# Full-width small operations in the norms, wider copies in S5, and a planner that looks 2000 operations ahead

## The chip, the cores and the metric

One core of a Trainium2 chip runs the whole program. The metric is the device time of one execution in microseconds (us); less is better. TensorE (PE) multiplies matrices out of SBUF into PSUM, which has eight banks of 128 partitions by 512 float32 values; VectorE (DVE), ScalarE (ACT) and GpSimd (POOL) do elementwise work on either memory; SyncE (SP) issues the DMA transfers. PE's weight loads have a line of their own, PEld.

## What is computed

Two blocks for a sequence of 512 tokens with 1024 features, in float32. The first is NSA attention (compressed, selected and windowed) beside retention, then a squared-ReLU feed-forward. The second is modulated by a condition vector (six gates out of `w_ada`), mixes with mLSTM beside an S5 state-space model, and ends with a gated feed-forward. What the change touches, cut from the reference:

```python
def rms_norm(x, w):
    xf = x.astype(jnp.float32)
    y = xf * lax.rsqrt(jnp.mean(xf * xf, axis=-1, keepdims=True) + EPS)
    return (y * w.astype(jnp.float32)).astype(x.dtype)

def _standardize(x):
    xf = x.astype(jnp.float32)
    mu = jnp.mean(xf, axis=-1, keepdims=True)
    var = jnp.mean(jnp.square(xf - mu), axis=-1, keepdims=True)
    return ((xf - mu) * lax.rsqrt(var + LN_EPS)).astype(x.dtype)

def _hybrid_mixer(h, ...):
    ...
    hm = _mlstm_chunkwise(q, k, v, ip.transpose(0, 2, 1), fp.transpose(0, 2, 1))
    hm = _standardize(hm).transpose(0, 2, 1, 3).reshape(Bsz, S, MLSTM_WIDTH).astype(h.dtype)
    y_a = (hm * mlstm_norm_gain * jax.nn.sigmoid(om)) @ w_mlstm_down
    ys = jax.nn.gelu(_s5_ssm(us, ...))
    ...

def _s5_ssm(u, ...):
    ...
    _, _, xr, xi = lax.associative_scan(combine, (a_r, a_i, bu_r, bu_i), axis=1)
    y = jnp.einsum('gcp,bsgp->bsgc', c_re, xr) - jnp.einsum('gcp,bsgp->bsgc', c_im, xi)
    y = y.reshape(Bsz, S, W) + d * uf
```

## The kernel before, in words

Activations lie with features on the partitions and tokens along the row: eight tiles `x` of 128 features by 512 tokens, worked on in halves `hf` of 256 tokens. A product in float32 is made as three products of rounded parts (`xh`, `xl` against `w` and its remainder); their matmuls write the PSUM tiles `ps_g`. Other PSUM tiles are `ps_s`, `ps_t` (transposes and broadcasts) and `ps_o`; all come from one pool of eight banks.

The program is not issued in the order in which it is written. A class `Order` records every operation with its dependences, and `flush` runs a list scheduler (`simulate`) several times with different priorities, each engine taking the most urgent of its operations that are ready; the best order is then issued engine by engine. What sets the order is therefore a table of costs: `time` (duration of an operation by engine, width and number of one-column operands), `shares` (whether DVE and POOL exclude one another in it), `region` (which part of a tile an operation touches) and `AHEAD`: no operation is issued that lies more than `AHEAD` places beyond the first one that is still to be issued. Since all operations are issued in one place, each has the same line, L519, and is told apart by its tiles.

The places that matter here:

- `newton` computes a reciprocal square root on DVE from an integer estimate and three steps. `rsqrt` scales its input. Results and temporaries are called `r..y`, `r..a`, `r..t`, with `rl` in the layer norms, `r1` and `r3` in the RMS norms, `rm` in mLSTM, `rq` and `rk` in the head norms. For four columns or fewer, every step is one operation for each column.
- A layer norm needs the mean over the partitions. `token_means` multiplies by a `mean` matrix into `ps_s`, copies the result to `tm` and transposes it; `add_up` has added most of the eight tiles (`ssum`, `lsum`) and of their squares (`sq`) before, but not tiles 6 and 7, so four tiles go through the `mean` matmuls. Then DVE copies the means (`lm`), forms the variance (`lw`, `lv`) and the root `rly`, and PE transposes `lm` and `rly` (the transposes `ps_t<-cf,lm` and `ps_t<-cf,rly`) into rows that DVE and POOL apply to `x`.
- `standardize2` does two layer norms at once from the sums of six quantities (`wsel`, `wrow`, then `wa`): first mean and root, then a second mean `wm`, variance `wv` and root. PE meets two roots in each half.
- `mlstm_head` copies numerator and denominator of each of four row blocks out of `ps_o` into `nm`, normalizes by `md`, and standardizes `nm` with the root `rmy`; PE then transposes `nm`.
- The end of S5: for each of four quarters, eight small matmuls `ps_o<-U,s5k` and eight matmuls with a block-diagonal operand, `ps_o<-s5z,wraw`. POOL zeroes `s5z`; DVE copies the states `X` into its diagonal blocks, 32 values on 64 partitions at a time. `X` itself comes out of PSUM earlier by `X<-ps_o`. DVE also computes a one-column `gb`, which ACT needs for `om`, mLSTM's output gate.
- `raw`: the 48 loads of `w_ada` and the DVE products with the condition, `raw<-raw,silu`.

Of the kernel before, what the change touches and what calls it, by code (L numbers as in the profile page):

```python
# [15 lines left out]
I32 = mybir.dt.int32  # L16
# [7 lines left out]
AHEAD = 800  # L24
# [151 lines left out]
class Order:  # L176
# [41 lines left out]
    def region(ap, t):  # L218

        if t.psum:  # L220
            return 0, 128, 0, 1
# [9 lines left out]
    def add(self, engine, fn, args, kw):  # L231
        i, deps, use = len(self.ops), set(), {}
        for a, w in [(a, n == 0) for n, a in enumerate(args)] + [(a, k == "accum_out") for k, a in kw.items()]:
# [4 lines left out]
            r, keep = self.region(a, t), []  # L238
# [10 lines left out]
    def time(self, engine, fn, args, kw):  # L249
# [5 lines left out]
        cols = sum(self.width(a) == 1 for a in aps[1:]) if wide > 1 else 0  # L255
# [9 lines left out]
        if engine == "vector":  # L265
            return 68 + wide * (6.25 if fn == "reciprocal" else 1.042) + 61 * cols + 60 * ("accum_out" in kw)
# [23 lines left out]
    def shares(self, op):  # L290
# [231 lines left out]
class Kern:  # L522
# [1808 lines left out]
```

## Time and profile before

| | before |
|---|---|
| median of 3 runs (lowest, highest) | 1505.81 us (1504.4, 1506.77) |
| profiled execution | 1505.45 us |
| its span, from first to last instruction | 1503.3 us |
| mean granted clock of PE | 0.991 |
| PE, DVE, ACT, POOL busy | 97%, 75%, 46%, 38% of the span |
| chain that ended last | PE 86%, DVE 10%, DMA 2%, ACT 1% |

The span is what the trace covers; the rest of the execution's time lies around it. A share of busy time is a mean over stages that differ. [...] "Idle before" is the time in which an engine stood still before an instruction, with the one that released it.

### The profile page before, as it was taken

The numbers are of one execution on the slowest core, as the hardware profiler recorded it, in microseconds if no ns is written. First come the engines' busy times: TensorE is split into PE (matmuls) and PEld (weight loads), VectorE is DVE, ScalarE is ACT, GpSimd is POOL, SyncE is SP. The second block draws the span as 40 slices with busy tenths as digits, with TensorE's granted clock in tenths as the row PEclk, the third lists the DMA queues.
The fourth block names the chain that finished last, engine by engine and source line by source line (L and its number), as shares of the span: only waits on it lengthen the run. The fifth ranks groups of instructions, "written<-read, shape, count | busy, mean of one in ns | idle before, by whom it ended". The sixth has DMA issues, their size and how long they took to land.

```text
span 1503.3 us, 24351 instructions
## 1 busy us (share of the span) xinstructions
PE 1461.9 (97%) x8738; PEld 1221.4 (81%) x8738; DVE 1124.8 (75%) x2641; ACT 688.6 (46%) x1397; POOL 569.8 (38%) x583
## 2 busy tenths in 40 slices
PE   9999999999999999999999899999999999999996
PEld 6779656888888777899778777878888899998996
DVE  6896798998974674565887863656488999897886
ACT  6454465444333333453563354434265555454553
POOL 6332334240060660143186102120127357464635
PEclk9999999999999999999999899999999999999998
DMA  6731114858731533415313543345311133323331
GB/s 218 224 108 64 56 43 160 267 193 279 235 116 42 176 129 119 153 46 176 107 57 100 158 137 124 119 147 180 143 63 51 50 106 99 116 88 106 100 97 57
DMA packets 81065, 188.34 MB, mean 125 GB/s; under 512 B 18352, under 2 KB 28528, under 8 KB 80944
## 3 DMA queue, kind: packets, MB, share of 16 engines
q1 hardware_dynamic: 80944, 186.78, 38.5%
q8 instruction: 69, 1.13, 0.3%
q14 instruction: 52, 0.43, 0.1%
HBM read 168.70 MB, written 15.17 MB: 122 GB/s over the span
## 4 chain that ended last, share of the span: by engine, by line
PE 86%; DVE 10%; DMA 2%; ACT 1%; issue 1%; POOL 0%; SPq 0%; ACTq 0%; DVEq 0%; POOLq 0%
PE ps_g L519 72%; PE ps_s L519 6%; PE ps_o L519 5%; PE ps_t L519 3%; DVE s5z L519 1%; DVE w L519 1%; DVE x L519 1%; DVE rlt L519 1%; DMA wraw<-in_w_fg_dram 1%; DVE rly L519 0%; DVE r3t L519 0%; DVE rmt L519 0%; DMA wraw<-in_w_f_dram 0%; DVE r3y L519 0%; DMA wraw<-in_w_down_dram 0%
## 5 line engine op out<-in xcount | busy, mean ns | idle before, releaser
L519 DVE TENSOR_TENSOR w<-wraw,w 128x512 fp32r<-128x512 f32 (+2 forms) x390 | 321.3, 837 | 92.2 <-ACT w L519 87.8
L519 ACT ACTIVATE w<-wraw 128x512 fp32r<-128x512 f32 (+1 forms) x398 | 240.3, 609 | 318.0 <-PE ps_g L519 248.6
L519 PE MATMUL ps_g<-xsh,w 128*128 128x256 f32 (+1 forms) x1088 | 278.8, 338 | 2.6 <-DVE w L519 2.2
L519 PE MATMUL ps_g<-xh,w 128*128 128x512 f32 x736 | 240.2, 398 | 0.0
L519 PEld LDWEIGHTS ps_g<-xsh,w 128*128 128x128 f32 x1088 | 188.6, 190 | 28.7 <-DVE w L519 2.6
L519 PE MATMUL ps_g<-xsl,w 128*128 128x256 f32 (+1 forms) x544 | 182.6, 336 | 0.0
L519 PEld LDWEIGHTS ps_g<-xh,w 128*128 128x128 f32 x736 | 137.7, 188 | 33.6 <-issue 1.9
L519 PE MATMUL ps_g<-xl,w 128*128 128x512 f32 x368 | 145.9, 397 | 0.0
L519 PE MATMUL ps_g<-mdh,w 128*128 128x512 f32 (+1 forms) x480 | 143.7, 374 | 0.1
L519 POOL TENSOR_TENSOR x<-x,lc 128x256 f32<-128x256 f32 x72 | 52.6, 773 | 185.9 <-ACT lc L519 173.7
L519 PEld LDWEIGHTS ps_g<-xsl,w 128*128 128x128 f32 x544 | 103.3, 190 | 11.0
L519 PE MATMUL ps_g<-tfh,w 128*128 128x256 f32 x576 | 107.5, 281 | 0.9 <-DVE wo L519 0.4
L519 PEld LDWEIGHTS ps_g<-mdh,w 128*128 128x128 f32 x480 | 87.1, 188 | 17.9 <-issue 0.8
L519 PE MATMUL ps_g<-fmh,w 128*128 128x512 f32 (+1 forms) x332 | 101.4, 375 | 0.0
L519 PEld LDWEIGHTS ps_g<-tfh,w 128*128 128x128 f32 x576 | 89.7, 188 | 2.1 <-DVE wo L519 0.9
L519 PE MATMUL ps_g<-mdl,w 128*128 128x512 f32 (+1 forms) x240 | 89.6, 373 | 0.0
L519 PEld LDWEIGHTS ps_g<-xl,w 128*128 128x128 f32 x368 | 69.2, 188 | 15.6
L519 PE MATMUL ps_g<-tfl,w 128*128 128x256 f32 x288 | 78.0, 281 | 0.0
L519 POOL TENSOR_TENSOR ws<-wraw 128x512 f32<-128x512 f32 x36 | 57.1, 1591 | 51.7 <-DMA wraw<-in_w_fv_dram 27.2
L519 DVE SCALAR_TENSOR_TENSOR raw<-raw,silu 128x1024 f32<-128x1024 f32 x48 | 62.7, 1305 | 9.7 <-DMA raw<-in_w_ada_dram 9.2
L519 PEld LDWEIGHTS ps_g<-fmh,w 128*128 128x128 f32 x332 | 59.8, 188 | 10.3 <-issue 0.2
L519 DVE TENSOR_TENSOR w<-ws,w 128x512 fp32r<-128x512 f32 x72 | 58.7, 829 | 11.1 <-ACT w L519 10.8
(510 smaller groups left out, 3471.1 us busy)
## 6 DMA issues: line engine op xcount, KB each, us to landing
raw<-in_w_ada_dram SPq DMA_DIRECT2D x48, 512.0 KB, 4.3
wraw<-in_w_dram SPq DMA_DIRECT2D x36, 512.0 KB, 3.7
wraw<-in_w_up_dram SPq DMA_DIRECT2D x32, 512.0 KB, 4.2
wraw<-in_w_down_dram SPq DMA_DIRECT2D x32, 512.0 KB, 3.7
wraw<-in_w_fv_dram SPq DMA_DIRECT2D x22, 512.0 KB, 3.9
wraw<-in_w_fg_dram SPq DMA_DIRECT2D x22, 512.0 KB, 3.7
wraw<-in_w_f_dram SPq DMA_DIRECT2D x14, 512.0 KB, 4.3
wraw<-in_w_fd_dram SPq DMA_DIRECT2D x16, 384.0 KB, 3.1
```

Source lines behind the costliest of these rows:

```text
L519: getattr(getattr(self.nc, op.engine), op.fn)(*op.args, **op.kw)
```

## The change

1. The planner: `AHEAD` goes from 800 to 2000. Dependences through a PSUM bank are kept by the whole bank for PE alone and by ranges for the other engines. One-column operations with column operands are planned at a higher cost, others at a lower one, and `shares` no longer exempts one-column operations or those that write PSUM.
2. `newton` always works on the full width, 11 operations in a row, and holds its value in PSUM (`room`): the upper half of the bank that `token_means` transposed into, the bank of the six sums in `standardize2`, or one more bank in `head_factors` and `mlstm_head`.
3. `standardize2` works on both columns at once with an operand in PSUM, and takes one square on ACT. mLSTM's `md` is formed for each row block, from PSUM.
4. `add_up` adds tiles 6 and 7 as well, so that two tiles, not four, go through the `mean` matmuls: 32 fewer on PE (8381 before, 8349 after), and two more additions for each sum on DVE or POOL.
5. S5: 64 copies of 64 values that are written next to each other take the place of 128 copies of 32 values written 32 bytes apart; the 8 memsets of 128x512 become 16 of 64x256. PE now reads `U` in steps of 32 bytes, and `s5z` in runs of eight values; ACT writes its result `y` in steps of eight values.

In instructions, DVE goes from 2595 to 2286, POOL from 588 to 604, ACT from 1335 to 1339 and its table loads from 4 to 6; SP's transfers are 492 in both.

```diff
 SLOTS = 70
-AHEAD = 800
+AHEAD = 2000
 NEG = -1.0e30
...
     @staticmethod
-    def region(ap, t):
-
-        if t.psum:
-            return 0, 128, 0, 1
+    def region(ap, t, bank=True):
+
+        if t.psum and bank:
+            return 0, 128, 0, S
         dims, o = [(int(s), int(c)) for s, c in ap.ap], int(ap.offset)
...
 
-        cols = sum(self.width(a) == 1 for a in aps[1:]) if wide > 1 else 0
+        cols = sum(self.width(a) == 1 for a in aps[1:]) if wide > 1 else sum(hasattr(a, "tensor") for a in (
+            args[2:4] if fn == "tensor_scalar" else args[2:3] if fn == "scalar_tensor_tensor" else kw.values()))
         if engine == "tensor":
...
             return len(aps) > 0
-        if op.engine != "vector" or any(a.tensor.name in self.psum for a in [op.args[0], *aps]):
+        if op.engine != "vector" or any(a.tensor.name in self.psum for a in aps):
             return False
-        one = self.width(op.args[0]) == 1
-        return op.fn in ("tensor_tensor", "scalar_tensor_tensor") or op.fn in ("tensor_scalar", "tensor_copy") and not one
+        return op.fn in ("tensor_tensor", "scalar_tensor_tensor") or op.fn in ("tensor_scalar", "tensor_copy") and op.args[0].tensor.name not in self.psum
 
...
         V = self.nc.vector
-        y, a, t = (self.small(name + c, n, bufs) for c in "yat")
-        if n <= 4:
-
-            y_, a_, t_, v_ = ([x[:, j:j + 1] for j in range(n)] for x in (y, a, t, v))
-            for j in range(n):
-                V.tensor_scalar(y_[j].bitcast(I32), v_[j].bitcast(I32), -0.5, float(0x5F3759DF), op0=OP.mult, op1=OP.add)
-                V.tensor_scalar(a_[j], v_[j], -0.5, None, op0=OP.mult)
-            for i in range(3):
-                for j in range(n):
-                    V.tensor_scalar(t_[j], y_[j], y_[j], a_[j], op0=OP.mult, op1=OP.mult)
-                for j in range(n):
-                    V.tensor_scalar(y_[j], t_[j], 1.5, y_[j], op0=OP.add, op1=OP.mult)
-            if post:
-                for j in range(n):
-                    V.tensor_scalar(y_[j], y_[j], post, None, op0=OP.mult)
-            return y
+        out, a, t = (self.small(name + c, n, bufs) for c in "yat")
+        y = self.room[:, 0:n]
         V.tensor_scalar(y.bitcast(I32), v.bitcast(I32), -0.5, float(0x5F3759DF), op0=OP.mult, op1=OP.add)
         V.tensor_scalar(a, v, -0.5, None, op0=OP.mult)
-        for _ in range(3):
-            V.tensor_tensor(t, y, y, op=OP.mult)
-            V.tensor_tensor(t, t, a, op=OP.mult)
-            V.scalar_tensor_tensor(y, t, 1.5, y, op0=OP.add, op1=OP.mult)
+        for i in range(3):
+            V.tensor_tensor(t, a, y, op=OP.mult)
+            V.tensor_tensor(t, t, y, op=OP.mult)
+            V.scalar_tensor_tensor(out if i == 2 and not post else y, t, 1.5, y, op0=OP.add, op1=OP.mult)
         if post:
-            V.tensor_scalar(y, y, post, None, op0=OP.mult)
-        return y
+            V.tensor_scalar(out, y, post, None, op0=OP.mult)
+        return out
 
...
         T.transpose(pt[:, 0:128], t, self.ident)
+        self.room = pt[:, 256:512]
         return pt[:, 0:128].rearrange("p (q r) -> p q r", r=32)[:, :, 0]
...
         n = st.n
+        self.room = self.bank("t")
 
...
         e = (self.nc.gpsimd, self.nc.vector)[k % 2]
-        if 1 < k < 6:
+        if k > 1:
             e.tensor_tensor(s[k % 2][:, c], (x[k - 2] if k < 4 else s[k % 2])[:, c], x[k][:, c], op=OP.add)
         self.nc.scalar.activation(q[k][:, c], x[k][:, c], AF.Square)
-        if 1 < k < 6:
+        if k > 1:
             e.tensor_tensor(q[k % 2][:, c], q[k % 2][:, c], q[k][:, c], op=OP.add)
...
             T.matmul(pv[:, 6 * j:6 * j + 6], rows[:, 128 * j:128 * j + 128], st.sel, start=j == 0, stop=True, skip_group_check=True)
-        a = self.small("wa", 12, 2).rearrange("p (n j) -> p n j", j=2)
-        V.tensor_copy(a, pv[:, 0:12].rearrange("p (j n) -> p n j", j=2))
-        m, s1, s2, s3, q, q2 = (a[:, n] for n in range(6))
+        m0, s1, s2, s3, q, q2 = (pv[:, 0:12].rearrange("p (j n) -> p n j", j=2)[:, n] for n in range(6))
+        m = self.small("wa", 2, 2)
+        V.tensor_copy(m, m0)
         c1, c2, c3, c4 = (st.cs[:, n:n + 1] for n in range(4))
-        v = self.small("wv", 2, 2)
-        each_ = lambda *vs: [[u[:, j:j + 1] for u in vs] for j in range(2)]
-        for m_, v_, q_ in each_(m, v, q):
-            V.tensor_scalar(v_, m_, m_, -1.0, op0=OP.mult, op1=OP.mult)
-        for m_, v_, q_ in each_(m, v, q):
-            V.tensor_scalar(v_, v_, 1e-5, q_, op0=OP.add, op1=OP.add)
+        v, t = self.small("wv", 2, 2), self.small("wt", 2, 2)
+        self.room = pv[:, 256:512]
+        V.scalar_tensor_tensor(v, m0, -1.0, m, op0=OP.mult, op1=OP.mult)
+        V.scalar_tensor_tensor(self.room[:, 2:4], q, 1e-5, v, op0=OP.add, op1=OP.add)
         mb = self.columns(m)
...
         A.activation(mc, mb, AF.Copy)
-        r = self.newton(v, 2, "rl")
-
-        for m_, a1, a2, a3, p_ in each_(m, s1, s2, s3, q2):
-            V.tensor_scalar(a1, m_, c1, a1, op0=OP.mult, op1=OP.subtract)
-            V.tensor_scalar(a3, m_, c3, a3, op0=OP.mult, op1=OP.subtract)
-            V.tensor_scalar(a2, m_, c2, a2, op0=OP.mult, op1=OP.subtract)
-            V.tensor_scalar(p_, a2, m_, p_, op0=OP.mult, op1=OP.add)
-            V.tensor_scalar(p_, a1, a1, p_, op0=OP.mult, op1=OP.subtract)
+        r = self.newton(self.room[:, 2:4], 2, "rl")
+
+        V.scalar_tensor_tensor(s1, m, c1, s1, op0=OP.mult, op1=OP.subtract)
+        V.scalar_tensor_tensor(s3, m, c3, s3, op0=OP.mult, op1=OP.subtract)
+        V.scalar_tensor_tensor(v, m, c2, s2, op0=OP.mult, op1=OP.subtract)
+        A.activation(t, s1, AF.Square)
+        V.tensor_tensor(s2, v, m0, op=OP.mult)
+        V.tensor_tensor(v, t, s2, op=OP.subtract)
+        V.tensor_tensor(q2, q2, v, op=OP.subtract)
         for k in range(8):
...
             A.activation(nm[i], po[:, 0:257], AF.Copy)
+            V.scalar_tensor_tensor(d0[:, i:i + 1], po[:, 256:257], -1.0, nm[i][:, 256:257], op0=OP.mult, op1=OP.max)
             st = self.small("bst", 6, 2)
...
 
-        d, e = self.small("md", 4, 2), self.small("me", 4, 2)
-        for i, t in enumerate(n2):
-            dn = t[:, :, 256]
-            V.scalar_tensor_tensor(d[:, 2 * i:2 * i + 2], dn, -1.0, dn, op0=OP.mult, op1=OP.max)
-        V.tensor_tensor(d, d, self.em[:, :, h], op=OP.max)
-        V.tensor_tensor(d, d, d, op=OP.mult)
+        self.room = self.bank("t")
+        d, e = self.room[:, 8:12], self.room[:, 4:8]
+        for t in (d, dm):
+            V.tensor_tensor(t, d0, self.em[:, :, h], op=OP.max)
+        V.tensor_tensor(d, d, dm, op=OP.mult)
         V.scalar_tensor_tensor(e, d, 1e-5, mv[:, :, 1], op0=OP.mult, op1=OP.add)
-        r = self.rsqrt(e, 4, 1.0, 0.0, "rm")
+        r = self.newton(e, 4, "rm")
         for i in range(4):
...
                 o = ps[:, 64 * g:64 * g + 64]
-                T.matmul(o, kk[g], self.U[q][:, g, :], start=g == 0, stop=False, skip_group_check=True)
+                T.matmul(o, kk[g], self.U[q][:, g, :].rearrange("p (s j) -> p j s", j=8), start=g == 0, stop=False, skip_group_check=True)
             for i in range(2):
-                x = self.t2("s5z", F32, (128, 4, 2, 64))
-                G.memset(x, 0.0)
+
+                x = self.t2("s5z", F32, (128, 2, 8, 4, 8))
                 for e in range(2):
                     r = slice(64 * e, 64 * e + 64)
+                    G.memset(x[r, 1 - e], 0.0)
                     for n in range(4):
-                        for j in range(2):
-                            V.tensor_copy(x.rearrange("p g e (s j) -> p j e g s", j=8)[r, 2 * n + j, e],
-                                          self.X[n][r, j, :, i, 4 * q:4 * q + 4].rearrange("p s g -> p g s"))
+                        V.tensor_copy(x[r, e, 2 * n:2 * n + 2], self.X[n][r, :, :, i, 4 * q:4 * q + 4].rearrange("p j s g -> p j g s"))
                 for g in range(4):
-                    T.matmul(ps[:, 128 * g:128 * g + 128], m[:, i, g, :], x[:, g].rearrange("p e k -> p (e k)"),
+                    T.matmul(ps[:, 128 * g:128 * g + 128], m[:, i, g, :], x[:, :, :, g, :],
                              start=False, stop=i == 1, skip_group_check=True)
             y = self.t2("y5")
-            A.activation(y, ps, AF.Copy)
+            A.activation(y.rearrange("p (g s j) -> p g j s", g=8, s=8), ps.rearrange("p (g j s) -> p g j s", g=8, j=8), AF.Copy)
             nc.sync.dma_start(yd[q].rearrange("s c g k -> (s c) (g k)"), y)
```

The change also moves instructions. Three places follow, the rows of one engine before and after, in the order in which they are issued; "x" at a row's end counts like rows in succession.

DVE at the end of one of mLSTM's heads and of S5, before: the last step of the root `rmy`, the scaling of `nm`, then copies into `s5z`, with `gb` behind 58 of them.

```order
L519 TENSOR_SCALAR rmy<-rmt,rmy 128x1 x4
L519 TENSOR_SCALAR nm<-nm,mv,rmy 128x256 x4
L519 COPY s5z<-X 64x4x8 x58
L519 TENSOR_SCALAR gb<-nw_899 128x1
L519 COPY s5z<-X 64x4x8 x2
L519 SCALAR_TENSOR_TENSOR om<-om,ps_t 128x512
L519 COPY s5z<-X 64x4x8 x2
```

The same place in the changed kernel.

```order
L521 COPY s5z<-X 64x64
L521 TENSOR_TENSOR rmt<-rma,ps_t 128x4
L521 TENSOR_SCALAR gb<-nw_894 128x1
L521 TENSOR_TENSOR rmt<-rmt,ps_t 128x4
L521 SCALAR_TENSOR_TENSOR ps_t<-rmt,ps_t 128x4
...
L521 SCALAR_TENSOR_TENSOR rmy<-rmt,ps_t 128x4
L521 TENSOR_SCALAR nm<-nm,mv,rmy 128x256 x4
L521 COPY s5z<-X 64x64 x32
L521 SCALAR_TENSOR_TENSOR om<-om,ps_t 128x512 x2
```

`gb` stands among the steps of the root, ahead of `nm` and of the 32 remaining copies; both `om` operations stand behind the copies.

PE in the first half of `standardize2`, inside the products `ps_g` of the feed-forward before: from `ps_t<-wsel,wrow` to the first root's transpose, `ps_t<-cf,rly`.

```order
L519 MATMUL ps_g<-ysh,w 128x256
L519 MATMUL ps_t<-wsel,wrow 128x6 x2
L519 MATMUL ps_g<-ysl,w 128x256
L519 MATMUL ps_g<-ysh,w 128x256 x2
...
L519 MATMUL ps_t<-cf,wa 128x128 x2
L519 MATMUL ps_g<-ysl,w 128x256
L519 MATMUL ps_t<-xr,meanr 128x256
L519 MATMUL ps_g<-ysh,w 128x256 x2
...
L519 MATMUL ps_g<-ysh,w 128x256
L519 MATMUL ps_t<-cf,rly 128x128 x2
```

The same place in the changed kernel.

```order
L521 MATMUL ps_g<-ysh,w 128x256
L521 MATMUL ps_t<-wsel,wrow 128x6 x2
L521 MATMUL ps_g<-ysl,w 128x256
...
L521 MATMUL ps_t<-xr,meanr 128x256
L521 MATMUL ps_g<-ysl,w 128x256
...
L521 MATMUL ps_t<-cf,wa 128x128 x2
L521 MATMUL ps_g<-ysh,w 128x256
...
L521 MATMUL ps_s<-x_2134,wsum 32x256
...
L521 MATMUL ps_s<-sq,wsum 32x256 x2
L521 MATMUL ps_g<-ysh,wkh 128x256
...
L521 MATMUL ps_t<-cf,rly 128x128
```

Between `wsel` and `rly` there were 24 products of 256 columns, and there are 52 now; the next half's `wsum` matmuls stand there as well.

DVE in the last layer norm of the program, from the copy of the means `lm` to the root's last step, before.

```order
L519 COPY lm<-ps_t 128x2
L519 SCALAR_TENSOR_TENSOR lw<-ps_t,lm 128x2
L519 SCALAR_TENSOR_TENSOR lv<-ps_t,lw 128x2
L519 TENSOR_SCALAR rly<-lv 128x1
L519 TENSOR_SCALAR rla<-lv 128x1
...
L519 TENSOR_SCALAR rlt<-rly,rla 128x1
L519 TENSOR_TENSOR x_2142<-x_2142,ps_t 128x256
L519 TENSOR_SCALAR rlt<-rly,rla 128x1
L519 TENSOR_SCALAR rly<-rlt,rly 128x1
L519 TENSOR_TENSOR x_2144<-x_2144,ps_t 128x256
...
L519 TENSOR_SCALAR rlt<-rly,rla 128x1 x2
L519 TENSOR_SCALAR rly<-rlt,rly 128x1 x2
```

The same place in the changed kernel.

```order
L521 COPY lm<-ps_t 128x2
L521 SCALAR_TENSOR_TENSOR lw<-ps_t,lm 128x2
L521 SCALAR_TENSOR_TENSOR ps_t<-ps_t,lw 128x2
L521 TENSOR_SCALAR ps_t<-ps_t 128x2
L521 TENSOR_SCALAR rla<-ps_t 128x2
L521 TENSOR_TENSOR x_2135<-x_2135,ps_t 128x256
L521 TENSOR_TENSOR rlt<-rla,ps_t 128x2
L521 TENSOR_TENSOR x_2137<-x_2137,ps_t 128x256
L521 TENSOR_TENSOR rlt<-rlt,ps_t 128x2
L521 TENSOR_TENSOR x_2139<-x_2139,ps_t 128x256
L521 SCALAR_TENSOR_TENSOR ps_t<-rlt,ps_t 128x2
...
L521 SCALAR_TENSOR_TENSOR rly<-rlt,ps_t 128x2
```

The one-column operations, which stood in pairs, are now one each, and the four subtractions from `x` stand between the first steps.

Beyond these places the larger `AHEAD` moves the `raw` products: of the 48, 3 stood ahead of the last maximum of attention's softmax (`mx`) in DVE's order, and 16 do now.

## Rows read from the trace of the kernel before

**Rows 1.** The page, part 1: busy time and share of each engine.
```profile
PE 1461.9 (97%) x8738; PEld 1221.4 (81%) x8738; DVE 1124.8 (75%) x2641; ACT 688.6 (46%) x1397; POOL 569.8 (38%) x583
```

**Rows 2.** Waits of PE, whole span: who released it, total us, times, longest.
```profile
PE ps_t L519 <- DVE rly L519: 10.7, 8, 3.5
PE ps_t L519 <- DVE nm L519: 5.1, 3, 2.4
PE ps_o L519 <- ACT om L519: 4.2, 1, 4.2
...
PE ps_t L519 <- DVE r3y L519: 1.6, 2, 1.1
...
PE ps_t L519 <- DVE wv L519: 0.8, 1, 0.8
PE ps_o L519 <- POOL s5z L519: 0.8, 1, 0.8
```

**Rows 3.** Timeline from 1489.9 us: start, duration, engine, operation, idle before and releaser.
```profile
1489.94 0.41 PE L519 MATMUL ps_s<-sq,mean 128*32 128x128 f32 x4
...
1491.12 0.16 DVE L519 COPY lm<-ps_t 128x2 f32<-128x2 f32 x1 [0.42 <-PE ps_t L519]
1491.31 0.16 DVE L519 SCALAR_TENSOR_TENSOR lw<-ps_t,lm 128x2 f32<-128x2 f32 x1
...
1495.26 0.69 PE L519 MATMUL ps_t<-cf,rly 128*128 128x128 f32 x2 [3.50 <-DVE rly L519]
```

**Rows 4.** Windows: PE, PEld, DVE, ACT, POOL busy; granted clock, DMA share, GB/s.
```profile
846.00:854.00 8.00, 6.70 (x31) 6.71 (x32) 7.42 (x23) 5.34 (x10) 2.30 (x2) 0.50 0.22 66
...
889.00:893.00 4.00, 4.00 (x12) 3.10 (x13) 3.87 (x9) 0.72 (x1) 0.00 (x0) 0.57 0.44 131
```

**Rows 5.** Timeline of DVE, ACT and PE from 829.5 to 847.3 us.
```profile
829.58 1.61 PE L519 MATMUL ps_o<-U,s5k 128*128 128x64 f32 x13
...
830.64 0.15 DVE L519 TENSOR_SCALAR rmy<-rmv 128x1 int32<-128x1 int32 x1
...
834.77 1.05 DVE L519 TENSOR_SCALAR nm<-nm,mv,rmy 128x256 f32<-128x256 f32 x3
...
836.05 10.24 DVE L519 COPY s5z<-X 64x32 f32<-64x32 f32 x58
...
846.56 0.69 ACT L519 ACTIVATE om<-ps_g,gb 128x512 f32<-128x512 f32 x1 [8.63 <-DVE gb L519]
...
847.30 1.12 PE L519 MATMUL ps_o<-U,s5k 128*128 128x64 f32 x4 [4.18 <-ACT om L519]
```

**Rows 6.** Groups of instructions of DVE: count, busy us, mean ns of one.
```profile
L519 DVE SCALAR_TENSOR_TENSOR raw<-raw,silu 128x1024 f32<-128x1024 f32 x48 | 62.7, 1305 | 9.7 <-DMA raw<-in_w_ada_dram 9.2
...
L519 DVE COPY s5z<-X 64x32 f32<-64x32 f32 x128 | 23.5, 210 | 1.2
...
L519 DVE COPY X<-ps_o 128x64 f32<-128x64 f32 (+1 forms) x32 | 5.2, 212 | 11.1 <-PE ps_o L519 11.1
...
L519 DVE SCALAR_TENSOR_TENSOR md<-nm 128x2 f32<-128x2 f32 x8 | 1.2, 154 | 0.0
...
L519 DVE SCALAR_TENSOR_TENSOR lw<-ps_t,lm 128x2 f32<-128x2 f32 x4 | 0.6, 159 | 0.1
```

**Rows 7.** Timeline of DVE and PE from 1098.6 to 1102.7 us.
```profile
1098.62 0.16 DVE L519 COPY wa<-ps_t 128x12 f32<-128x12 f32 x1
...
1099.63 0.40 PE L519 MATMUL ps_g<-ysh,w 128*128 128x256 f32 x2
...
1099.99 0.40 PE L519 MATMUL ps_g<-ysh,w 128*128 128x256 f32 x2
...
1102.67 0.62 PE L519 MATMUL ps_t<-cf,rly 128*128 128x128 f32 x2 [0.97 <-DVE rly L519]
```

**Rows 8.** Windows of one stage of block 1 and one of block 2, columns as above.
```profile
200.00:262.00 62.00, 60.53 (x386) 37.22 (x384) 56.00 (x210) 35.03 (x109) 28.15 (x42) 1.00 0.36 116
...
1095.00:1202.00 107.00, 98.84 (x797) 91.69 (x796) 95.26 (x268) 62.59 (x133) 54.59 (x62) 1.00 0.18 58
```

More of the change, by code (lines that the diff above doesn't have):

```diff
@@ L237, in add @@
             use[a.tensor.name] = True
-            r, keep = self.region(a, t), []
+            r, keep = self.region(a, t, engine == "tensor"), []
             for j, q, wq in t.acc:
@@ L265, in time @@
         if engine == "vector":
+            if fn == "tensor_scalar" and not any(a.tensor.name in self.psum for a in aps) and aps[1].dtype == F32:
+                return 68 + 0.52 * wide + 61 * cols
             return 68 + wide * (6.25 if fn == "reciprocal" else 1.042) + 61 * cols + 60 * ("accum_out" in kw)
@@ L690, in rsqrt @@
     def rsqrt(self, ssum, n, scale, eps, name, post=None, bufs=2):
-        v = self.small(name + "v", n, bufs)
+        v = self.room[:, n:2 * n]
         if isinstance(eps, float):
@@ L1158, in scores @@
                 V.tensor_reduce(mx, ps[:, 0:n], axis=AX.X, op=OP.max, negate=True)
-                A.activation(P[g][:, o], ps[:, 0:n], AF.Exp, bias=mx, accum_out=den[:, i, br, g, r:r + 1])
-            d = den[:, i, br, :, r]
+                A.activation(P[g][:, o], ps[:, 0:n], AF.Exp, bias=mx, accum_out=den[:, i, br, r, g:g + 1])
+            d = den[:, i, br, r]
             V.reciprocal(d, d)
@@ L1321, in standardize @@
         tok = [slice(256 * hf + 128 * j, 256 * hf + 128 * j + 128) for j in range(2)]
-        pv = self.token_means([[u[:, tok[j]] for u in t] for t in ([*s, *x[6:]], [*q[0:2], *q[6:]]) for j in range(2)])
-        m, w, v = (self.small("l" + n, 2, 2) for n in "mwv")
+        pv = self.token_means([[t[i][:, tok[j]] for i in range(2)] for t in (s, q) for j in range(2)])
+        m, w = (self.small("l" + n, 2, 2) for n in "mw")
+        v = self.room[:, 2:4]
         V.tensor_copy(m, pv[:, 0:2])
-        V.scalar_tensor_tensor(w, pv[:, 0:2], -1.0, m, op0=OP.mult, op1=OP.mult)
         if isinstance(eps, float):
+            V.scalar_tensor_tensor(w, pv[:, 0:2], -1.0, m, op0=OP.mult, op1=OP.mult)
             V.scalar_tensor_tensor(v, pv[:, 2:4], eps, w, op0=OP.add, op1=OP.add)
         else:
-            V.tensor_tensor(v, pv[:, 2:4], w, op=OP.add)
-            for j in range(2):
-                V.tensor_scalar(v[:, j:j + 1], v[:, j:j + 1], eps[:, 2 * hf + j:2 * hf + j + 1], None, op0=OP.add)
+            V.scalar_tensor_tensor(v, pv[:, 0:2], -1.0, m, op0=OP.mult, op1=OP.mult)
+            V.tensor_tensor(w, pv[:, 2:4], eps[:, 2 * hf:2 * hf + 2], op=OP.add)
+            V.tensor_tensor(v, v, w, op=OP.add)
         mb = self.bank("t")
@@ L1438, in standardize2 @@
         rb = self.columns(r)
-        m2, v2 = self.small("wm", 2, 2), self.small("wv", 2, 2)
-        for v_, p_, r_, a3 in each_(v2, q2, r, s3):
-            V.tensor_scalar(v_, p_, r_, a3, op0=OP.mult, op1=OP.add)
-        for v_, r_ in each_(v2, r):
-            V.tensor_scalar(v_, v_, r_, -1.0, op0=OP.mult, op1=OP.mult)
-        for v_, in each_(v2):
-            V.tensor_scalar(v_, v_, c4, None, op0=OP.add)
-        for m_, a1, r_ in each_(m2, s1, r):
-            V.tensor_scalar(m_, a1, r_, -1.0, op0=OP.mult, op1=OP.mult)
-        r2 = self.newton(v2, 2, "rl")
+        m2, v2, w2 = self.small("wm", 2, 2), self.small("wv", 2, 2), pv[:, 272:274]
+        self.room = pv[:, 288:512]
+        V.scalar_tensor_tensor(m2, s1, -1.0, r, op0=OP.mult, op1=OP.mult)
+        V.tensor_tensor(v2, q2, r, op=OP.mult)
+        V.tensor_tensor(w2, v2, s3, op=OP.subtract)
+        V.tensor_tensor(v2, w2, r, op=OP.mult)
+        V.tensor_scalar(w2, v2, c4, None, op0=OP.add)
+        r2 = self.newton(w2, 2, "rl")
         mb = self.columns(m2)
@@ L2108, in mlstm_head @@
         mv = self.small("mv", 8, 2).rearrange("p (i a) -> p i a", i=4)
+        d0, dm = self.small("md", 4, 2), self.small("me", 4, 2)
         for i in range(4):
```

3 lines of the change are left out of this document (1 added, 2 removed).

## The prediction

> **What bounds the kernel now.** First the busy times [rows 1]: PE works 97% of the span, DVE 75%. A cheaper DVE or ACT operation is therefore worth nothing by itself. Time can come only from PE's idle time (1503.3 - 1461.9 = 41.4 us), from stretches in which its clock is granted by half, and from PE work that goes away. So I read next who PE waits for [rows 2]. The reader should see that five of the six names are results of the small operations which the diff rewrites: rly and wv (reciprocal roots and their relatives in the layer norms), nm (mLSTM's head norm), r3y (attention's key norm), s5z (S5's zero-padded blocks); om, the sixth, is shown below to stand behind the s5z copies. [...] Last the timelines of three such waits [rows 3, 5, 7] and the stages' windows [rows 8].
>
> The sum is made against the profiled execution, 1505.45 us (span 1503.3 and 2.15 us around it), which is 0.36 us under the median of 1505.81.
>
> **Reciprocal roots.** For four columns, the old form takes 32 one-column operations: from rmy at 830.64 to nm at 834.77 that is 4.13 us [rows 5], and PE waits for nm. The new form is 11 full-width operations, each waiting for the one before. The trace has no DVE operation that writes PSUM. The nearest row, lw, reads PSUM and depends on lm: they start 1491.12 and 1491.31, so 0.19 us a step [rows 3]. 11 x 0.19 = 2.1 us. The bounds are 0.154 a step, the duration of a two-wide operation wholly in SBUF (md, [rows 6]), which gives 1.7 us, and 0.38, a PSUM write as dear as two such steps, which gives 4.2 us, no gain. I take 0.19, since lw (159 ns) and md (154 ns) hardly differ. [...]
>
> **Layer norms (rly, wv).** Outside the tail, PE waits 10.7 - 3.5 + 0.8 = 8.0 us [rows 2]. Here the order counts as much as the chain. In the first of the second norm's halves, wa is copied at 1098.62 and PE can go on with rly at 1102.67, 0.97 us late [rows 7]. In the new order 52 wide matmuls stand between wsel and the first rly transpose, where 24 stood; three of them start every 0.36 us (1099.63 to 1099.99 [rows 7]), so the cover grows by 28 x 0.12 = 3.4 us. The stall comes back only if the new chain is longer by more than 0.97 less, that is 2.4 us over the old. The second root of that norm, and the second half of the plain one, gain less cover; I leave 1.1 us there, and take -6.9 (bounds 0 and -8.0).
>
> **The tail.** The 3.50 us before rly at 1495.26 has no PE work left to cover it. From lm to the transpose is 4.14 us; now lm, lw, the variance and 11 steps, 14 x 0.19 = 2.7, and four x subtractions of 256 columns that DVE does in between lengthen it by some 0.8 (half of 4 x 0.4, estimated as in the next sentence; the rest falls into the steps' own waits). Against it, the sum of squares gains an addition ahead of the last mean matmul, 256 columns wide, 0.4 us by my estimate (twice the 212 ns of X, 64 wide [rows 6]). -0.3 net (bounds -1.0 and +1.0).
>
> **Key norms in attention (r3y).** 1.6 us [rows 2], with the 4.1-us chain cut to 2.1 and more PE work ahead of the transposes: -1.4.
>
> **mLSTM (nm).** PE waits 5.1 us in three places [rows 2]. The chain gets 2 us shorter in each head; the waits were 1.2 to 2.4 long. -4.0, bounds 0 and -5.1.
>
> **S5.** PE's wait of 4.18 us at 847.30 is released by om on ACT, which itself waited 8.63 us for gb on DVE [rows 5]. Nothing makes gb late but the queue: 58 s5z copies stand ahead of it from 836.05, 10.24 us. In the new order gb stands before nm, ahead of those copies, so what is left is the copies themselves: the last quarter's 16 ahead of its matmuls. 128 copies of 210 ns [rows 6], started every 0.176 us (10.24 / 58), become 64 of twice the width. X, 64 wide, has 212 ns [rows 6], so I take 0.21 us: 13.4 us where 22.5 were; bounds 0.176 (11.3 us) and 0.352 (22.5 us, nothing gained). At 0.21 the 32 copies behind nm last 6.7 us and fit beside the transposes and PE's earlier quarters; at 0.35 some 3 us of the wait stay. With POOL's memset ahead of s5z (0.8) the term is -5.0, bounds 0 and -5.0.
>
> **The clock.** 6.70 us of PE work at half clock cost 3.35, and 4.00 at 0.57 cost 1.7 [rows 4]; both follow waits that go. -5.1, bounds 0 and -5.1.
>
> **Fewer mean matmuls.** 32 of them go. Four take 0.41 us from the first start to the last end [rows 3], at most 0.103 each and 3.3 us in all; the last one's whole pass through the pipeline is in that, so I take under half, 0.043 each: -1.4.
>
> **What it adds.** Two more table loads on ACT and 16 smaller memsets on POOL, engines at 46% and 38% [rows 1]. The reach of 2000 also brings 13 of the 48 raw operations (gates of block 2, 1.305 us each and 0.08 for their accumulator) ahead of the last softmax maximum of attention: 13 x 1.39 = 18 us of DVE work into a stretch where DVE is busy 56.0 of 62 us [rows 8]. The key norms' four roots give DVE back 4 x 2.0 = 8 us there, so 10 stay, and DVE was idle for 6. I take +3 for new gaps there and +1 elsewhere; bounds 0 and +18.
>
> **Sum.** 6.9 + 0.3 + 1.4 + 4.0 + 5.0 + 5.1 + 1.4 = 24.1 us off, 4 on: 1505.45 - 20.1 = 1485.4, rounded to 1485.
>
> **Rivals.**
> *The waits only move.* From 1095 to 1202 us DVE is busy 95.3 of 107 [rows 8]; a stage held by DVE's whole load does not get shorter because PE's work stands elsewhere. For it: the nm and rly waits lie in such stretches. Against: the roots' own DVE work drops there as well. Then only S5, its 3.35 us of clock and the matmuls count: 9.8, and the same 4 against them: 1499.6.
> *U read in steps.* The moving operand of U's 64 matmuls is now read in steps of 32 bytes. 13 take 1.61 us [rows 5], 0.12 each and 7.9 us in all. No row here has a moving operand with such a step; X, which DVE reads from PSUM in steps of 32 bytes, takes the 212 ns of the s5z copies of half its width [rows 6], and these matmuls take 1.9 ns a column, slow enough to hide a slow read. Twice as long gives 1493, four times 1508 (no change); from just over that it is slower. [...]
> *Banks held too long (slower).* PSUM has eight banks. The second norm now holds the bank of its means through both roots, about 13 us for each of two halves (52 wide matmuls make 6.2 of them); the four mLSTM heads and the two key and query norms take one more for about 3 us each, 18 in all. 44 us with a bank fewer; om above shows PE waiting for a bank (4.2 us). If PE stood still for 24 of the 44, the time would be 1509 and slower by 0.2%. Against: om is the only bank that PE waits long for [rows 2], and in the new order wide matmuls go on while the means' bank is held.
> *Attention's DVE.* All 18 us of raw fall on PE: 1485 + 15 = 1500.
> *No change.* The chip takes 0.38 a step and 0.35 a copy: the chains stay, and the terms for the clock and for waits go with them: about 1505.
>
> **Chances.** Forecast (1477 to 1493) 0.58; waits move or attention loaded (1494 to 1502) 0.22; U twice to three times 0.05, at four times 0.03; no change 0.05; banks 0.07. So 1476 to 1502 holds eight in ten. A change within 0.2% (3 us, about what three runs can tell from none) has 0.08, faster 0.85, slower 0.07.
>
> **What would show it.** In the profile after: rly, nm and om in PE's list of waits sum to 4 to 6 us, not 20; a wide root takes 2.1 us from first to last step; s5z copies are 64 of about 0.21 us; granted clock from 840 to 900 us near 1; the matmuls of U still start every 0.12 at most. The prediction is wrong if PE's busy time rises (U), if waits named ps_g for banks appear in the norms, or if attention's windows show PE under 95% with DVE full.

## The result and the profile after

The changed kernel takes 1479.36 us (median of 4 runs, 1478.5 to 1480.85) against 1505.13 us (4 runs): ratio 0.983, 95% interval [0.981, 0.985], 25.8 us less. The forecast was 1485 in a range of 1476 to 1502.

The page of the changed kernel, span and busy times, to be read against [rows 1].

```profile
span 1477.4 us, 23963 instructions
...
PE 1450.1 (98%) x8674; PEld 1216.2 (82%) x8674; DVE 1087.6 (74%) x2332; ACT 694.0 (47%) x1401; POOL 577.0 (39%) x599
```

PE's idle time is 1477.4 - 1450.1 = 27.3 us, 14.1 less than before; its busy time is 11.8 us less. Who PE waits for, in the columns of [rows 2].

```profile
PE ps_t L521 <- DVE rly L521: 4.0, 3, 3.2
PE ps_g L521 <- ACT wo L521: 3.4, 4, 1.2
PE ps_o L521 <- issue: 1.3, 1, 1.3
```

rly has lost 6.7 of 10.7 us, and nm, om, r3y and wv have left the list; the 0.8 us that stood under s5z are now the 1.3 under "issue", as the experiment on the planner's costs shows. What else stands there now is scattered: `wo` is a weight of the feed-forward, and five new names have one wait of 1.0 to 1.2 us each, among them `ce` and `vt`, operands of attention and mLSTM, and `lsum`, the sum ahead of the last norm. "Issue" is a wait of PE for which the trace has no releaser. The windows answer to [rows 4, 8]: PE's busy time is the first pair, the clock the third number from the end. The windows are the same by the clock, and so lie some 5 to 20 us further along in the program than before. The first line is of the kernel before, the others are of the changed one.

```profile
820.00:900.00 80.00, 71.42 (x372) 59.77 (x371) 60.23 (x259) 35.20 (x62) 9.02 (x12) 0.91 0.44 135
...
200.00:262.00 62.00, 61.75 (x386) 39.32 (x386) 56.23 (x208) 33.06 (x102) 27.71 (x39) 1.00 0.50 165
820.00:900.00 80.00, 78.72 (x429) 65.79 (x428) 48.57 (x152) 47.42 (x74) 14.53 (x23) 1.00 0.51 165
```

In the S5 stage PE worked 71.42 of 80 us at a clock of 0.91 and works 78.72 at 1.00 now. The 107 us from 1095 hold different parts of the program before and after, so for the second norm the same piece of work is compared: from the first `ps_t<-wsel,wrow` of the second norm to the first product `ps_g<-tfh,w` of the feed-forward, before and after.

```profile
1098.02:1178.67 80.65, 75.62 (x615) 70.12 (x613) 72.13 (x235) 50.84 (x110) 46.09 (x56) 1.00 0.16 53
...
1076.64:1151.46 74.82, 74.65 (x614) 69.90 (x613) 66.07 (x197) 49.76 (x110) 47.12 (x56) 1.00 0.18 58
```

PE's idle time in it went from 5.03 to 0.17 us and DVE's own work from 72.13 to 66.07. The S5 timeline answers to [rows 5].

```profile
822.77 0.15 DVE L521 TENSOR_SCALAR gb<-nw 128x1 f32<-128x1 f32 x1
...
823.86 1.46 DVE L521 TENSOR_SCALAR nm<-nm,mv,rmy 128x256 f32<-128x256 f32 x4
...
825.24 2.55 DVE L521 COPY s5z<-X 64x64 f32<-64x64 f32 x16
...
826.66 1.10 ACT L521 ACTIVATE y<-ps_o 128x512 f32<-128x512 f32 x1 [0.31 <-PE ps_o L521]
...
827.86 1.13 PE L521 MATMUL ps_o<-s5z,wraw 128*128 128x128 f32 x8 [1.28 <-issue]
```

`gb` comes at 822.77, ahead of `nm`, and `om` no longer holds PE. The copies are short, 16 in 2.55 us. What is left is the 1.28 us before PE goes on at 827.86. Two things end just ahead of that, ACT's first `y` at 827.76 and 16 copies at 827.79; the experiment on the planner's costs tells which of them it is. The root of mLSTM's last head is now this:

```profile
957.43 0.16 DVE L521 TENSOR_SCALAR rma<-ps_t 128x4 f32<-128x4 f32 x1
957.62 0.16 DVE L521 TENSOR_TENSOR rmt<-rma,ps_t 128x4 f32<-128x4 f32 x1
...
959.37 1.38 DVE L521 TENSOR_SCALAR nm<-nm,mv,rmy 128x256 f32<-128x256 f32 x4
```

From `rma` at 957.43 to `nm` at 959.37 is 1.94 us for ten steps of 0.19: 2.1 with the estimate ahead of it, where the old root took 4.13. In the S5 stage, where copies into s5z stand between its steps, a root takes 3.2 us (820.70 to 823.86).

### The profile page after: what moved, and what is told of

It is laid out like the page before. It is cut to its first block, busy times and chain, and to the rows that moved or that the text cites. A ratio compares the mean times of both kernels' runs of the same rounds, so it can differ in the third digit from the quotient of the medians.

```text
span 1477.4 us, 23963 instructions
## 1 busy us (share of the span) xinstructions
PE 1450.1 (98%) x8674; PEld 1216.2 (82%) x8674; DVE 1087.6 (74%) x2332; ACT 694.0 (47%) x1401; POOL 577.0 (39%) x599
## 5 line engine op out<-in xcount | busy, mean ns | idle before, releaser
L521 PEld LDWEIGHTS ps_g<-xl,w 128*128 128x128 f32 x368 | 69.3, 188 | 15.7 <-issue 0.2
L521 DVE TENSOR_TENSOR w<-ws,w 128x512 fp32r<-128x512 f32 x72 | 66.9, 947 | 10.1 <-ACT w L521 9.6
L521 PEld LDWEIGHTS ps_g<-fmh,w 128*128 128x128 f32 x332 | 60.5, 188 | 10.2 <-issue 0.2
L521 ACT ACTIVATE w<-ws 128x512 fp32r<-128x512 f32 x72 | 45.4, 631 | 46.3 <-PE ps_g L521 38.5
```

Source lines behind the costliest of these rows:

```text
L521: getattr(getattr(self.nc, op.engine), op.fn)(*op.args, **op.kw)
```

## The experiments

Where not said otherwise an experiment starts from the changed kernel. Medians are of 4 runs (10 in the column roots' first run). The kernel before was run beside them in three groups and took 1505.29 us (reach of 800, reach of 2000 before, old norms, old S5), 1503.55 (column roots, room in SBUF, four tiles, old costs) and 1505.19 (the other reaches, columns in the same order). The changed kernel was not run again, so differences from its 1479.36 us carry up to 2 us from one group to another.

### The planner's reach

```diff
-AHEAD = 2000
+AHEAD = 800
```

> The changed kernel with the planner's reach back at 800, nothing else changed. Theory of the waits (the time went with PE's waits for the roots, for om and with the half clock behind them; the reach only shuffles): 1480 to 1484 us, waits for rly outside the tail under 2 us. Theory of the reach (2000 is what puts enough PE work ahead of each root): 1490 us or more, with rly and r3y back in PE's list of waits with 5 us or more.

1489.4 us, ratio to before 0.989 [0.988, 0.991]. Neither expectation held whole: 10 us were lost, but not at the roots, rly outside the tail being 0.7 us. In this order `w` is late at the start of the first feed-forward.

```profile
411.75 3.21 ACT L521 ACTIVATE w<-wraw 128x512 fp32r<-128x512 f32 x6
...
412.41 0.80 PE L521 MATMUL ps_g<-mdh,w 128*128 128x512 f32 x1 [2.32 <-ACT w L521]
```

ACT's roundings of `w` begin only at 411.75; PE waits 2.32 us and then 1.35 at 414.98, and the clock, 0.50 from 412 to 416 us and 0.64 in the next 4, takes some 2.5 us more out of 6.24 us of work. What half clock costs PE can be read in the kernel before: 16 matmuls `ps_o<-s5z,wraw` take 2.00 us at 839.33, where the clock is 1.00, and 3.73 at 850.76, where it is 0.50. Two more stretches at half clock follow, from 728 and from 1204 us (some 3.3 us of PE's time), and the wait for lsum in the tail is 2.5 us, not 1.05. Reaches of 1400 and 3000 tell whether that is a trend.

> The changed kernel with a reach of 1400. If reach as such is worth the 10 us between 800 and 2000: in between, 1482 to 1487 us. If the planner's orders scatter and the reach is no cause: anywhere from 1477 to 1492 us, without a trend to the run at 3000.

> The changed kernel with a reach of 3000. If reach as such is the cause: 1476 to 1480 us, no worse than 2000. If orders scatter: anywhere from 1477 to 1492 us.

1480.47 us at 1400 and 1480.14 at 3000 (both 0.983 to 0.984 [0.982, 0.985]), as at 2000; the first lies under the 1482 to 1487 us that a trend would give. So from 1400 to 3000 the reach does nothing. At 800 the order loses 10 us in the places above; why the planner makes such an order there was not settled. In the kernel before, the reach goes the other way.

```diff
-AHEAD = 800
+AHEAD = 2000
```

> The kernel before with a reach of 2000, nothing else changed. Theory of the waits: 1500 to 1506 us, since no chain gets shorter; nm and om still make PE wait 7 us or more. Theory of the reach: 1493 us or less, with rly under 5 us in PE's list.

> The kernel before with a reach of 1400. If reach as such harms the kernel before (1516 us at 2000): 1507 to 1514 us. If orders scatter: anywhere from 1498 to 1518 us; in both cases PE waits 7 us or more for rly, and nm stays in its list.

1516.5 us at 2000 (ratio 1.007 [1.006, 1.009]) and 1513.37 at 1400 (1.006 [1.004, 1.007]). The first is slower than either theory said; the second lies in both ranges and decides nothing by itself. PE's waits at 2000.

```profile
PE ps_t L519 <- DVE rly L519: 10.2, 8, 3.5
PE ps_t L519 <- DVE nm L519: 3.7, 2, 2.1
```

rly waits as before (10.2 for 10.7 us) and nm almost (3.7 for 5.1): with the old chains a larger reach covers little. Why it loses 8 to 11 us was not settled; the extra time is partly in PE's busy time (1468.4 us, 6.5 more), partly in scattered waits.

### The planner's costs, and S5 alone

With `time` and `shares` as before, all else changed:

> The changed kernel with the costs of operations and the rule on DVE and POOL as before; reach 2000 and dependences by range kept. Theory of the waits: the wide roots need little planning, 1479 to 1483 us. Rival, the planner's costs: 1487 us or more, with roots in PE's list.

1478.59 us, ratio 0.983 [0.981, 0.985]: the costs are worth nothing here. This trace also tells what PE waits for in S5.

```profile
825.30 2.63 DVE L519 COPY s5z<-X 64x64 f32<-64x64 f32 x16
...
827.14 1.09 ACT L519 ACTIVATE y<-ps_o 128x512 f32<-128x512 f32 x1 [0.31 <-PE ps_o L519]
...
828.34 1.13 PE L519 MATMUL ps_o<-s5z,wraw 128*128 128x128 f32 x8 [1.28 <-issue]
```

The copies are done at 827.93 and `y` at 828.23, and PE goes on at 828.34. In each of the 13 traces that have this wait PE goes on 0.10 us after the end of ACT's first `y`, to within rounding, while the last copy ends 0 to 4.4 us ahead of it; with the old S5, where `y` takes 0.60 us, the wait is 0.78 us (827.95 and 828.05). In the kernel before it is the 0.79 us at 832.94 that the list puts down to POOL's s5z, and `y` ends at 832.84. So `y` ends it by the times, though no trace names it. The kernel before with the new costs, the dependences by range, a new layout of attention's softmax sums and the new S5, but old norms and the reach of 800:

> The kernel before with the changed planner costs and the changed end of S5, but with the norms, roots and sums of before and the reach of 800. Theory of the waits: S5's term alone, 5.0 us of waits and 3.35 us of half clock, so 1496 to 1498 us; rly and nm stay in PE's list with 10 us or more together. Rival, the planner's costs (one-column operations were planned too cheap, and the true cost is what hides them): 1488 us or less, rly and nm under 6 us together.

1517.05 us, ratio 1.007 [1.005, 1.009]; both expectations failed. The old S5 stall at om is gone from its list, as it should be, but the new order has other stalls; nm still has 2.4 us.

```profile
PE ps_g L521 <- DVE w L521: 6.3, 4, 3.8
PE ps_g L521 <- ACT xsh L521: 5.3, 1, 5.3
PE ps_s L521 <- DVE lsum L521: 4.0, 1, 4.0
```

The 5.3 us behind `xsh`, 3.8 of the 6.3 behind `w` and 4.0 behind `lsum` are single waits that the kernel before does not have, and half clock costs PE twice as much (PE's busy time times the missing share of the clock, summed over windows of 4 us, is 14.6 us for 7.2). Parts cannot be priced by adding them to the kernel before: any edit draws a new order, and such an order can lose more than the part gains. The tests below therefore take one part out of the changed kernel, and one of them keeps its order.

### S5 as before

```diff
-                        V.tensor_copy(x[r, e, 2 * n:2 * n + 2], ...)
+                        for j in range(2):
+                            V.tensor_copy(x.rearrange("p g e (s j) -> p j e g s", j=8)[r, 2 * n + j, e], ...)
```

> The changed kernel with the end of S5 as before: 128 copies of 32 values, U and y contiguous. Theory of the waits: the 5.0 us of waits and 3.35 us of half clock come back, 1486 to 1489 us, and om or s5z stands in PE's list with 3 us or more. Rival (the order alone, gb ahead of the copies, took the wait away, and the copies are hidden either way): 1478 to 1481 us.

1486.92 us, ratio 0.988 [0.986, 0.990], 7.6 us more than the changed kernel, as the theory of the waits had it. Timeline, and the window behind the wait.

```profile
831.71 0.15 DVE L521 TENSOR_SCALAR gb<-nw 128x1 f32<-128x1 f32 x1
831.88 10.36 DVE L521 COPY s5z<-X 64x32 f32<-64x32 f32 x58
...
836.12 1.89 PE L521 MATMUL ps_o<-U,s5k 128*128 128x64 f32 x16
...
843.08 0.55 PE L521 MATMUL ps_t<-rr,pick 64*128 64x256 f32 x1 [2.43 <-DVE s5z L521]
```

```profile
844.00:852.00 8.00, 8.00 (x37) 7.66 (x37) 5.33 (x14) 7.72 (x15) 3.43 (x4) 0.50 0.76 231
```

58 copies take 10.36 us again. This time `gb` is ahead of them, so that order alone does not help: PE waits 2.43 us for them at another place, and 8 us of PE's work right behind run at 0.50, which is 4 us. The rival falls. The planner drew this order anew too, but PE's differs from the changed kernel's in only 61 of 8674 places, none of them ahead of 727 us.

### The roots

Column by column again, planned as such:

> The changed kernel, but each root of up to four columns is again computed column by column, in SBUF (16 or 32 operations); all else as changed. Theory of the waits: a four-column root takes 4.1 us, not 2.2, and a two-column one some 0.5 us more; nm and r3y come back in PE's list, 1484 to 1490 us. Rival (the planner covers the longer chain once its costs are right): 1479 to 1481 us.

1507.88 us, slower even than before (1.003 [1.002, 1.004]), far above both expectations. The page of this run:

```profile
PE 1470.0 (98%) x8674; PEld 1225.2 (81%) x8674; DVE 1114.7 (74%) x2573; ACT 695.3 (46%) x1401; POOL 576.4 (38%) x599
```

PE is busy 20 us longer on the same 8674 matmuls, and half clock, behind waits of 3.3 and 4.8 us among other places, accounts for some 8 of them by the same sum. The rest was not settled. The order is another one: the block that neighbouring matmuls use of the array changes its size 312 times in this trace and 244 in the changed kernel's, but what that costs was not measured. So the next run keeps the order: the planner sees the 11 wide operations, and the column operations are put in their places when the program is issued.

```diff
+                for fn, args, kw in self.alt.get(i, [(op.fn, op.args, op.kw)]):
+                    getattr(getattr(self.nc, op.engine), fn)(*args, **kw)
...
+                alt[N + 3 + 3 * i] = [ts(c(t, j), c(out, j), c(out, j), c(a, j), op0=OP.mult, op1=OP.mult) for j in J]
+                alt[N + 4 + 3 * i] = [ts(c(out, j), c(t, j), 1.5, c(out, j), op0=OP.add, op1=OP.mult) for j in J]
```

> The changed kernel with every engine's order kept as it is, but each root of up to four columns issued column by column in SBUF, as before: 16 or 32 one-column operations stand where the 11 full-width ones stood. Theory of the waits: PE waits for rly, nm and r3y come back, some 2 us for each four-column root (8 of them and one r1) as far as PE's work does not cover it, and 0.3 to 1 us for each two-column one, with half clock behind the longest: 1487 to 1495 us. Theory of the planner (column roots are harmless in this order, the 28 us of the earlier run were a bad order): 1479 to 1483 us.

1495.03 us, ratio 0.993 [0.992, 0.995]: 15.7 us more than the changed kernel (the upper end expected was 1495), with 244 changes of shape as there. PE's waits, and the timeline of mLSTM's last head.

```profile
PE ps_t L522 <- DVE rly L522: 7.4, 7, 3.7
PE ps_t L522 <- DVE r3y L522: 2.9, 3, 1.4
...
PE ps_g L522 <- DVE r3y L522: 1.6, 1, 1.6
```

```profile
969.66 0.35 DVE L522 TENSOR_SCALAR rmy<-ps_t 128x1 int32<-128x1 int32 x4
...
973.83 1.37 DVE L522 TENSOR_SCALAR nm<-nm,mv,rmy 128x256 f32<-128x256 f32 x4
...
974.38 0.41 PE L522 MATMUL ps_t<-cf,nm 128*128 128x128 f32 x2 [1.91 <-DVE nm L522]
```

The root takes 4.17 us again (969.66 to 973.83), and PE waits 1.91 us for nm; the r3y waits in attention, which the changed kernel has none of, sum to 4.5 us. This is the cleanest measure of the form of the roots, in an order drawn for the short ones: some 16 of the 26 us. The theory that the planner's new order made most of the gain falls. With the 7.6 us of S5, 23 of the 26 us are taken back by two tests that keep or nearly keep the order. The two-column form of `standardize2`, the new `md` and the dependences by range were not taken out alone.

### PSUM or SBUF

```diff
-        self.room = pt[:, 256:512]
+        self.room = self.small("room", 64, 4)
```

> The changed kernel with the roots' values in SBUF in place of PSUM; same 11 operations, no extra bank held. If PSUM as an operand only matters for the length of one operation: within 2 us of the changed kernel, 1478 to 1481 us, roots as long as before. Rival (with both operands in SBUF DVE's steps are held up by POOL's work, as the 24-wide key root of the kernel before, 550 ns a step): 1482 to 1488 us, and the steps beside POOL work take 300 ns or more.

1492.81 us, ratio 0.992 [0.990, 0.995]: 13.4 us more, beyond even the rival. One root of the second norm, on DVE beside POOL, and two groups: the first with the shortest, median and longest duration in ns, the second with the mean.

```profile
1127.77 0.66 DVE L521 TENSOR_TENSOR rlt<-rlt,room 128x2 f32<-128x2 f32 x1
...
1130.95 4.45 POOL L521 TENSOR_SCALAR x<-x 128x512 f32<-128x512 f32 x7
1131.07 0.56 DVE L521 TENSOR_TENSOR rlt<-rlt,room 128x2 f32<-128x2 f32 x1
...
1134.39 0.66 PE L521 MATMUL ps_t<-cf,rly 128*128 128x128 f32 x2 [5.54 <-DVE rly L521]
```

```profile
L521 DVE TENSOR_TENSOR rlt<-rlt,room x24: 146/216/1247, 653.5 to 1481.0; 128x2 f32<-128x2 f32 x24
...
L521 DVE TENSOR_TENSOR rmt<-rmt,room 128x4 f32<-128x4 f32 x12 | 1.9, 161 | 0.4
```

`rlt<-rlt,room` takes 0.66 us at 1127.77 beside POOL's `ws` and `sq`, and 0.56 at 1131.07 beside the `x` operations; in mLSTM, where POOL works for 0.62 of the 9.5 us around the four roots in the changed kernel's trace, the same step is 0.161. The changed kernel's row for it, with the other operand in PSUM:

```profile
L521 DVE TENSOR_TENSOR rlt<-rlt,ps_t x24: 146/150/158, 652.6 to 1469.0; 128x2 f32<-128x2 f32 x24
```

All 24 take 0.146 to 0.158 us there; with the room in SBUF they take 0.146 to 1.247. So the operand in PSUM is no detail: without it PE waits 11.0 us for rly, 7.0 more. Not every step beside POOL is as long: `rlt<-rla,room` takes 0.18 us at 1132.90, beside the `x` operations. What holds DVE up in the others the trace does not name. The planner drew a new order for this kernel as well, so that not all of the 13.4 us need be this.

### Four tiles through the mean matmuls

> The changed kernel with add_up and the means as before: tiles 6 and 7 go through the mean matmuls themselves, 32 more matmuls. By the sum of the forecast: the matmuls cost 1.4 us of PE, the tail gets back 0.4 us; 1480 to 1481 us. Rival (the additions ahead of the last means, 1.05 + 0.45 us of waits for lsum and sq in the tail, cost as much as the matmuls save): 1478 to 1479.5 us.

1479.85 us, ratio 0.983 [0.982, 0.985], the changed kernel's time within its spread and between the two ranges, so that it decides for neither. Its tail, and that of the changed kernel.

```profile
1462.70 0.30 PE L521 MATMUL ps_s<-lsum,mean 128*32 128x128 f32 x2
```

```profile
1463.23 0.41 PE L521 MATMUL ps_s<-lsum,mean 128*32 128x128 f32 x4 [1.05 <-POOL lsum L521]
...
1469.41 0.69 PE L521 MATMUL ps_t<-cf,rly 128*128 128x128 f32 x2 [3.22 <-DVE rly L521]
```

With four tiles the sums are there when PE comes to them (1462.70, 0.2 after the last product starts); with two PE waits 1.05 us for lsum and, at 1464.09, 0.45 for sq. The matmuls of the tile `mean` are 198 records of 12.4 us here and 134 of 10.6 us in the changed kernel, so what they save, 1.8 us, is about given back in the tail. The order is new from 16 us on, with 2.5 us of waiting for `w` that the changed kernel does not have, so the equal times by themselves do not show that balance.

## Why the prediction was right, and where it was not

**What bounds the kernel: right.** Time came only from PE's idle time, 14.1 us where 17.6 off and 4 on make 13.6, and from its busy time, 11.8 where 6.5 was forecast: 6.9 of them are the clock and some 2 the mean matmuls, by the paragraphs below, and the other 3 stay unassigned.

**Roots: size right, reason incomplete.** A step takes 0.19 us with PSUM written, as taken from lw; a four-column root 2.1 us where nothing stands between its steps, as forecast. But lw and md were read as showing that PSUM and SBUF are alike. md stands where POOL does little (POOL is idle beside seven of the eight `md<-nm`, which take 0.13 to 0.15 us, and works beside the one at 793.88, which takes 0.22), and lw has only one operand in SBUF. Beside POOL, the SBUF-only steps shown above take three and a half to four times as long, and the SBUF room costs 13.4 us with its order. The 24-wide key root in the trace of before would have told it: of its three steps `rkt<-rkt,rka` the one beside POOL took 1.30 us and the others 0.17 and 0.18.

**Layer norms, key norms, nm: right.** rly outside the tail and wv fell from 8.0 to 0.8 us (forecast 1.1 left), r3y from 1.6 to 0, nm from 5.1 to 0 (forecast 1.1 left). The cover argument for the second norm came out by a hair, and not as it was meant. Its first half has no rly wait:

```profile
1077.24 0.15 DVE L521 COPY wa<-ps_t 128x2 f32<-128x2 f32 x1
...
1084.06 0.14 DVE L521 SCALAR_TENSOR_TENSOR rly<-rlt,ps_t 128x2 f32<-128x2 f32 x1
...
1084.26 0.33 PE L521 MATMUL ps_t<-cf,rly 128*128 128x128 f32 x1
```

But from wa to the transpose it is 7.02 us now where it was 4.05, 3.0 more, beyond the 2.4 that were to bring the wait back. The planner put other DVE work (roundings of `w`, subtractions from `x`) between the root's steps, and rly ends 0.06 us before PE comes to it. With PE's order kept and column roots the wait is there, with all the cover:

```profile
1099.59 0.32 PE L522 MATMUL ps_t<-cf,rly 128*128 128x128 f32 x1 [0.62 <-DVE rly L522]
```

So cover alone was not enough here; the shorter root was needed.

**S5: right in kind, 1.3 us too large.** om's wait went. The 0.8 us put down to s5z did not: the sum took them for POOL's memset, but they end with ACT's first `y`, and that write takes 1.10 us now for 0.60, so that the wait grew to 1.28. The writes of `y` in steps of eight values had no term in the sum. Copies start every 0.16 us (16 in 2.55), under the 0.21 taken. Taken out again, S5 costs 7.6 us, wait and clock together, for the 8.4 in the sum (5.0 and 3.35).

**The clock: the term was too small.** I priced two stretches, 5.1 us; there was a third, with PE never idle:

```profile
732.00:736.00 4.00, 4.00 (x30) 3.70 (x29) 3.90 (x16) 2.16 (x4) 0.00 (x0) 0.93 0.30 116
736.00:740.00 4.00, 4.00 (x15) 2.82 (x15) 2.19 (x11) 0.42 (x2) 0.00 (x0) 0.65 0.42 131
```

It cost 1.7 us, and the changed kernel has no half clock before the tail. By the sum over windows of 4 us, half clock costs PE 7.2 us before and 0.3 after. Half clock followed waits of 4.18 us (om, to 847.30) and 2.36 (nm, to 888.34) in the kernel before, and of 2.43 with the old S5. A wait does not decide it alone: near 1155 us PE waits 2.52 us for `w` with the reach of 1400 and with four tiles, and half clock follows (0.63 and 0.66 from 1156 to 1160 us); with the reach of 3000 it waits 2.53 us there and the clock stays at 1.00. The stretch at 735 had no such wait ahead of it, only some two microseconds of matmuls of 4 to 16 columns; what ended it was not tried.

**The tail and the mean matmuls: both mis-sized, with a sum near nothing.** rly's wait went from 3.50 to 3.22 us, but lsum and sq added 1.5 us, not 0.4. The sum priced 32 matmuls by rows of the trace, but the 32 of the program are 64 records there: the busy time of the tile `mean` fell from 12.8 to 10.6 us, 2.2 and not 1.4, which about pays for lsum and sq.

**New gaps: 4 us, wrong in place, the size luck.** The raw products did not hurt attention: PE works 61.75 of 62 us there, 60.53 before. The gaps that came are wo (3.4, 0.7 before), ce, vt, mdh and xch (1.0 to 1.2 each), 7.1 us more in all; older scattered waits, such as P (1.4), went. Net of the waits accounted for above some 2 us are left, and no reason given for the 4 has to do with either.

**The rivals.** *The waits only move* fell: in the second norm and its products, with DVE at 89%, PE's idle time went from 5.03 to 0.17 us, and DVE's own work fell by 6 us there. *U in steps*: 16 matmuls with contiguous U take 1.89 us (836.12 in the run with the old S5), and in steps of 32 bytes, in the changed kernel:

```profile
836.06 2.06 PE L521 MATMUL ps_o<-U,s5k 128*128 128x64 f32 x16
```

2.06 us, so 0.011 us each, 0.7 us in all: a penalty of a tenth, not of two or four times. *Banks held too long* did not show: no bank wait of PE is tied to a root. *No change* and *attention's DVE* fell with the result.

## What to carry to other kernels

Where one engine is busy 97% of the time, read its list of waits by name, add what the clock lost behind them where the windows show it, and price the chains that end them; here that sum came within 6 us of a change of 26, with terms missed in both directions. A releaser named in such a list can be the wrong one: compare the end times over several runs. Small operations on DVE that a waiting engine depends on should have one operand in PSUM if GpSimd works beside them, as the rows with the room in SBUF show (0.56 and 0.66 us a step beside POOL, 0.146 to 0.158 with PSUM). Where a planner draws the order anew, compare parts with the order held fixed, or the order's own scatter of some 10 us hides them.

## What was not expected of the hardware

ACT's four writes of y in steps of eight values took 1.14 us each, against 0.60 in the run with the old S5 (contiguous, second line):

```profile
L521 ACT ACTIVATE y<-ps_o 128x512 f32<-128x512 f32 x4 | 4.6, 1141 | 0.3 <-PE ps_o L521 0.3
...
L521 ACT ACTIVATE y<-ps_o 128x512 f32<-128x512 f32 x4 | 2.4, 596 | 1.4 <-PE ps_o L521 1.4
```

By the times above, the first of the four stands in PE's way: its 0.5 us more are the growth of PE's wait from 0.79 to 1.28 us. Behind the other three PE does not wait. In these runs the step of 32 bytes thus cost ACT's write 0.55 us on 0.60 and PE's 16 matmuls with U 0.17 us on 1.89.
